# A decoder trunk on one core: output projections that hold the activations and move 512 weight columns, and norms with tokens on partitions

## The chip, the core and the metric

The kernel runs on one core of a Trainium2 chip. The metric is the device time of one execution in microseconds, taken as the median of several runs. The engines are TensorE (PE, with its weight loads as PEld), VectorE (DVE), ScalarE (ACT), GpSimd (POOL), and SyncE (SP), which here only issues DMAs.

## The reference

The input is 256 tokens of 2048 channels in float32. Two post-norm layers follow each other. Each of the four sub-steps has the same frame:

```python
x = layer_norm(alpha * x + mixer(x) @ w_out, g, b)   # alpha = 4 ** 0.25
x = layer_norm(alpha * x + conv_ffn(x), g, b)        # up, causal conv, gate, down
```

The even layer's mixer is a state-space scan beside block-sparse attention; the odd layer's is a three-branch sparse attention beside retention. Both end in a 2048 x 2048 output projection. The feed-forward part is 5632 wide, so its down projection is 5632 x 2048. `layer_norm` takes mean and variance over the 2048 channels of a token, with float32 throughout.

## The kernel before

**Products.** Every float32 operand of a projection is split in a high part and a rest, and three products are summed: high by high, high by rest, rest by high. Activations of a projection lie with channels on partitions, `[128, k, 512]`: 256 tokens of the high part, then 256 of the rest. The weights come from HBM in slabs of up to 128 x 1024 (`prep`); ACT makes the high part (L105, `whi`), DVE the rest (L106, `wlo`). Four buffers each hold the raw slab and the two parts, and slabs are prepared three ahead of their use.

**Forms of a projection.** In form B (`group_b`, L237) the weights stand in TensorE, 128 x 128, and 512 columns of activations move past the high part, 256 past the rest, for two blocks of 128 output channels. In form A (`group_a`, L266 to L268) 128 tokens of activations stand and up to 512 weight columns move, three matmuls for each token half. Form S (`group_one`, L191 to L193) is B for one block of 128 with three moves of 256.

**Output projections and norms.** There are four (`out_proj`): after the even mixer (16 k), the first down projection (44 k), after the odd mixer (16 k), the second down projection (44 k). Each has seven B groups of 256 output channels and two S groups of 128. The residual `r` lies with channels on partitions, so a norm needs sums over partitions: `token_sums` (L345) multiplies by a column of 1/2048, early for the first 15 blocks and once more for the last. `norm` then spreads mean (L359) and inverse deviation (POOL's power, L368, and L359 again) over partitions by transposes, and goes block by block: subtract the mean (L378), scale (L387), high part of `x` on ACT (L401), rest on DVE (L403). The blocks behind the first two are applied inside the next stage's first group (`apply_to`). At norm 3 each block gets its bias on ACT (L396) and is stored (L397), 16 stores of 128 KB.

**Order.** A scheduler orders each engine's instructions from the program order and its own estimates; `Fill` hands small steps to the projections' loops, a few after each k. The DMAs of SP go in one queue in program order. At the start SP issues x in eight pieces between the weight slabs, then the constants (`ident`, `prm`, `tri`, then `oh` at L459 and `mk`), and then more slabs, the sixteenth first; the matmul L463 on `oh` makes the position bias.

## Time and profile before

| | us |
|---|---|
| median of 3 runs | 2350.85 (2349.8 to 2352.26) |
| the profiled execution's span | 2351.1 |
| TensorE busy in it | 2321.1 |
| VectorE busy | 1460.5 |
| ScalarE busy | 1160.9 |
| output projection 0, first matmul to last | 286.59 to 382.89 |
| output projection 1 | 882.67 to 1129.80 |
| output projection 2 | 1490.77 to 1587.22 |
| output projection 3 | 2087.20 to 2334.33 |

The profiled execution lies 0.25 us above the median, so its rows stand for the runs. A row's second number is the length of that row: of one instruction, or of several that follow each other with the same operands, counted by x. Matmuls overlap in the records, so the pace is read from start to start, not from a row's length. An idle time in brackets stands before its row, with what ended it.

### The profile page before, as it was taken

The numbers are of one execution on the slowest core, as the hardware profiler recorded it, in microseconds if no ns is written. First come the engines' busy times: TensorE is split into PE (matmuls) and PEld (weight loads), VectorE is DVE, ScalarE is ACT, GpSimd is POOL, SyncE is SP. The second block draws the span as 40 slices with busy tenths as digits, with TensorE's granted clock in tenths as the row PEclk, the third lists the DMA queues.
The fourth block names the chain that finished last, engine by engine and source line by source line (L and its number), as shares of the span: only waits on it lengthen the run. The fifth ranks groups of instructions, "written<-read, shape, count | busy, mean of one in ns | idle before, by whom it ended". The sixth has DMA issues, their size and how long they took to land.

```text
span 2351.1 us, 34466 instructions
## 1 busy us (share of the span) xinstructions
PE 2321.1 (99%) x13638; PEld 2043.2 (87%) x13638; DVE 1460.5 (62%) x2095; ACT 1160.9 (49%) x1556; POOL 20.8 (1%) x29
## 2 busy tenths in 40 slices
PE   9999999999999999999999999999999999999997
PEld 9888888888888888889789888888888888888887
DVE  5677667766666664555645667768666666655555
ACT  5554544655555554444545553446555555544443
POOL 0001000000000000000000000000000000000000
PEclk9999999999999999999999999999999999999999
DMA  7664554655555555555656634455555555555553
GB/s 239 196 192 148 160 169 145 205 187 188 190 190 185 192 189 191 188 188 178 186 168 223 195 108 153 162 176 168 192 189 189 188 188 188 188 190 190 188 190 112
DMA packets 124674, 426.30 MB, mean 181 GB/s; under 512 B 13872, under 2 KB 18400, under 8 KB 124384
## 3 DMA queue, kind: packets, MB, share of 16 engines
q1 hardware_dynamic: 124512, 424.09, 54.0%
q8 instruction: 107, 1.75, 0.3%
q14 instruction: 55, 0.45, 0.1%
HBM read 421.93 MB, written 2.11 MB: 180 GB/s over the span
## 4 chain that ended last, share of the span: by engine, by line
PE 87%; issue 10%; DVE 1%; DMA 1%; ACT 0%; SPq 0%; POOL 0%; ACTq 0%; POOLq 0%; DVEq 0%
PE acc L237 74%; PE acc L266 2%; PE acc L267 2%; PE acc L268 2%; PE ps L237 1%; PE acc L191 1%; PE acc L192 1%; PE acc L193 1%; PE ps L568 1%; DVE r L387 0%; PE ps L507 0%; DMA wraw<-in_ev_in 0%; PE ps L534 0%; DMA r<-in_x 0%; DMA oh<-in_c_onehot 0%
## 5 line engine op out<-in xcount | busy, mean ns | idle before, releaser
L106 DVE TENSOR_TENSOR wlo<-wraw,whi 128x1024 fp32r<-128x1024 f32 (+4 forms) x818 | 973.2, 1191 | 645.4 <-ACT whi L105 642.7
L105 ACT ACTIVATE whi<-wraw 128x1024 fp32r<-128x1024 f32 (+4 forms) x818 | 843.3, 1032 | 793.0 <-PE acc L237 613.6
L237 PE MATMUL acc<-x,whi 128*128 128x512 f32 x3840 | 1202.6, 399 | 3.4 <-DVE x L403 3.4
L237 PEld LDWEIGHTS acc<-x,wlo 128*128 128x128 f32 x3840 | 707.4, 189 | 158.5 <-issue 0.2
L237 PE MATMUL acc<-x,wlo 128*128 128x256 f32 x3840 | 741.0, 279 | 0.0
L237 PEld LDWEIGHTS acc<-x,whi 128*128 128x128 f32 x3840 | 595.9, 190 | 16.3 <-DVE x L403 3.9
L237 PE MATMUL acc<-g,whi 128*128 128x512 f32 x1232 | 385.3, 396 | 0.0
L237 PEld LDWEIGHTS acc<-g,wlo 128*128 128x128 f32 x1232 | 229.9, 188 | 52.9
L237 PE MATMUL acc<-g,wlo 128*128 128x256 f32 x1232 | 240.4, 278 | 0.0
L237 PEld LDWEIGHTS acc<-g,whi 128*128 128x128 f32 x1232 | 188.8, 189 | 1.2
L280 ACT ACTIVATE tmp<-acc 128x512 f32<-128x512 f32 x120 | 71.6, 596 | 216.2 <-PE acc L237 216.2
L237 PE MATMUL acc<-y,whi 128*128 128x512 f32 x448 | 140.9, 399 | 0.0
L266 PE MATMUL acc<-whi,x 128*128 128x512 f32 (+4 forms) x288 | 101.1, 351 | 1.9 <-ACT x L401 1.1
L267 PE MATMUL acc<-wlo,x 128*128 128x512 f32 (+4 forms) x288 | 100.9, 350 | 0.0
L268 PE MATMUL acc<-whi,x 128*128 128x512 f32 (+4 forms) x288 | 100.3, 349 | 0.0
L237 PEld LDWEIGHTS acc<-y,wlo 128*128 128x128 f32 x448 | 82.0, 188 | 18.0
L237 PE MATMUL acc<-y,wlo 128*128 128x256 f32 x448 | 86.5, 280 | 0.0
L1017 DVE SCALAR_TENSOR_TENSOR c<-fpad,prm,c 128x256 f32<-128x256 f32 x176 | 73.9, 480 | 1.4 <-ACT c L1014 1.3
L237 PEld LDWEIGHTS acc<-y,whi 128*128 128x128 f32 x448 | 69.8, 189 | 1.6 <-DVE y L171 0.2
L283 DVE TENSOR_TENSOR u<-acc,tmp 128x512 f32<-128x512 f32 x44 | 30.5, 693 | 53.7 <-ACT tmp L280 53.7
L266 PEld LDWEIGHTS acc<-whi,x 128*128 128x128 f32 x288 | 55.5, 193 | 7.8 <-ACT x L401 1.5
L283 DVE TENSOR_TENSOR fpad<-acc,tmp 128x512 f32<-128x512 f32 x42 | 29.1, 692 | 51.6 <-ACT tmp L280 51.6
(290 smaller groups left out, 1548.0 us busy)
## 6 DMA issues: line engine op xcount, KB each, us to landing
wraw<-in_up SPq DMA_DIRECT2D x328, 512.0 KB, 3.3
wraw<-in_down SPq DMA_DIRECT2D x174, 512.0 KB, 3.3
wraw<-in_od_in SPq DMA_DIRECT2D x96, 512.0 KB, 3.5
wraw<-in_ev_in SPq DMA_DIRECT2D x72, 512.0 KB, 3.6
wraw<-in_ev_out SPq DMA_DIRECT2D x32, 512.0 KB, 3.5
wraw<-in_od_out SPq DMA_DIRECT2D x32, 512.0 KB, 3.3
wraw<-in_up SPq DMA_DIRECT2D x32, 384.0 KB, 3.0
wraw<-in_ev_in SPq DMA_DIRECT2D x16, 348.0 KB, 4.3
```

Source lines behind the costliest of these rows:

```text
L105: a = nc.scalar.activation(hi[:, :n], raw[:, :n], AF.Copy)
L106: b = nc.vector.tensor_tensor(lo[:, :n], raw[:, :n], hi[:, :n].bitcast(F32), op=OP.subtract)
L191: nc.tensor.matmul(acc, hi[:, kk, :], xh, start=(k == 0), stop=False)
L192: nc.tensor.matmul(acc, hi[:, kk, :], xl, start=False, stop=False)
L193: nc.tensor.matmul(acc, lo[:, kk, :], xh, start=False, stop=(k == nk - 1))
L237: nc.tensor.matmul(acc, wt, mv, start=(k == 0 and i < len(unit)), stop=(k == nk - 1 and i >= len(unit)))
L266: nc.tensor.matmul(o, xh, wh, start=(k == 0), stop=False)
L267: nc.tensor.matmul(o, xh, wl, start=False, stop=False)
L268: nc.tensor.matmul(o, xl, wh, start=False, stop=(k == KT - 1))
L280: nc.scalar.activation(t, a[:, :, 256:], AF.Copy, scale=sign)
L283: nc.vector.tensor_tensor(d, a[:, :, :256], t, op=OP.add)
L1017: nc.vector.scalar_tensor_tensor(c[:, i, :], pad[:, i, t:t + 256], w[:, t:t + 1], c[:, i, :], op0=OP.mult, op1=OP.add)
```

## The change

All four output projections go in four groups of 512 output channels, in form A: the activations of 128 tokens stand, 512 weight columns move, three matmuls for each token half and k. The residual `r` now has tokens on partitions, `[128, 2, 2048]`, and is loaded for that in one DMA of 2 MB, which SP issues behind `tri` and ahead of `oh`, `mk` and the slabs that follow. A group's evacuation is one addition per token half (L485, L487) with a partial statistic (L489, bn_stats), and the norm merges these (L188), makes the inverse deviation (L189 on DVE, L190 on POOL) and centres and scales 512 channels at once (L204).

In a projection's last group the last four slabs (8 k) are first multiplied for token half 0 only. Half 0's norm is issued then, and half 1 of the four slabs follows on TensorE. The normed values are turned to channels on partitions by transposes (`turn`, L238), four of 128 x 128 for each token half and 512 channels, 32 per norm. For the first 512 channels the evacuation is ACT (L247, high part) and DVE (L248 and L249, rest) per 128 channels; for the others ACT writes 4 x 128 (L253) and DVE makes high part and rest of all four at once (L255, L256). A table, `plan`, sets between which matmuls each turn stands: two in the half-1 pass, the others in the next stage's head, its first 8, 4 or 8 slabs, which are multiplied for half 0's tokens, then half 1's, then with the weights' rests (`head_b`). The head's slabs are prepared during the projection's groups, into memory that is free at that time (`home`). For norms 1 to 3 the residual `r` is first given its gain and bias again from rows broadcast to all partitions (8 DMAs per norm, two DVE operations of 128 x 1024 per group, L509 and L510). At norm 3 the blocks go by DVE (L214, L215) or by ACT and POOL (L223 to L225) to eight stores of 256 KB (L207).

```diff
+LEAD = 4
...
 def out_jobs(src, nk):
-    return [(src, "B", cols((256 * i, 256)), nk) for i in range(7)] + [
-        (src, "S", cols((1792 + 128 * i, 128)), nk) for i in range(2)]
+    return [(src, "A", cols((512 * i, 512)), nk) for i in range(4)]
...
+        self.plan = {("t1", LEAD - 2): [(0, 0)], ("t1", LEAD - 1): [(0, 1)]}
+        if idx in (0, 2):
+            self.plan.update({("h0", head - 3): [(1, 0)], ("h0", head - 1): [(1, 1)], ("h1", 1): [(0, 2)],
+                              ("h1", 4): [(0, 3)], ("h1", head - 1): [(1, 2)], ("lo", 3): [(1, 3)]})
...
+    def start(self, t):
+        T, nc = self.k, self.k.nc
+        mv, rs = self.mv[:, t, :], self.rs[:, t, :]
+        nc.vector.bn_aggr(mv, self.stats[:, t, :, :])
+        nc.vector.tensor_scalar(rs[:, 0:1], mv[:, 1:2], EPS, None, op0=OP.add)
+        nc.gpsimd.tensor_tensor(out=rs[:, 1:2], in0=rs[:, 0:1], in1=T.mhalf[:, 0:1], op=OP.pow)
+        if self.idx == 3:
+            nc.vector.tensor_scalar(self.nm[:, t:t + 1], mv[:, 0:1], rs[:, 1:2], -1.0, op0=OP.mult, op1=OP.mult)
+            self.finish_pool(t, 2 + t)
+            if t == 1:
+                self.finish(0, 3)
+            for c in range(2 + t):
+                self.finish(t, c)
+        else:
+            self.centre(t, 0)
+            self.centre(t, 1)
...
+    def turn(self, t, c):
+        T, nc = self.k, self.k.nc
+        if c > 1:
+            self.centre(t, c)
+        ps = T.ps()
+        for i in range(4):
+            nc.tensor.transpose(ps[:, 128 * i:128 * i + 128], T.r[:, t, 512 * c + 128 * i:512 * c + 128 * i + 128], T.ident)
+        g, b = T.lng[:, self.idx, :], T.lnb[:, self.idx, :]
+        x = T.x[:, 4 * c:4 * c + 4, :]
+        hi, lo = (x[:, :, 256 * j + 128 * t:256 * j + 128 * t + 128] for j in range(2))
+        y = T.rp.tile([128, 2, 256], F32, name="tmp", bufs=2).rearrange("p a (b c) -> p (a b) c", b=2)
+        if c == 0:
+            for i in range(4):
+                k = 4 * c + i
+                p = ps[:, 128 * i:128 * i + 128]
+                nc.scalar.activation(hi[:, i, :], p, AF.Identity, scale=g[:, k:k + 1], bias=b[:, k:k + 1])
+                nc.vector.tensor_scalar(y[:, i, :], p, g[:, k:k + 1], b[:, k:k + 1], op0=OP.mult, op1=OP.add)
+                nc.vector.tensor_tensor(lo[:, i, :], y[:, i, :], hi[:, i, :].bitcast(F32), op=OP.subtract)
+            return
+        for i in range(4):
+            k = 4 * c + i
+            nc.scalar.activation(y[:, i, :], ps[:, 128 * i:128 * i + 128], AF.Identity, scale=g[:, k:k + 1],
+                                 bias=b[:, k:k + 1])
+        nc.vector.tensor_copy(hi, y)
+        nc.vector.tensor_tensor(lo, y, hi.bitcast(F32), op=OP.subtract)
...
+        for t in range(2):
+            for k in range(n):
+                for u in order:
+                    for o, acc in enumerate(units[u]):
+                        c = 256 * u + 128 * o
+                        nc.tensor.matmul(half(acc, t), slabs[k][0][:, 0, c:c + 128], half(act[k], t),
+                                         start=(k == 0 and t == 0), stop=False)
+                self.turns.at(f"h{t}", k)
+        for k in range(n):
+            for u in order:
+                for o, acc in enumerate(units[u]):
+                    c = 256 * u + 128 * o
+                    nc.tensor.matmul(acc[:, :256], slabs[k][1][:, 0, c:c + 128], act[k][:, :256], start=False, stop=False)
+            self.turns.at("lo", k)
...
+    def three(self, o, a, t, wh, wl, first, last):
+        nc = self.nc
+        xh, xl = a[:, t * 128:(t + 1) * 128], a[:, 256 + t * 128:256 + (t + 1) * 128]
+        nc.tensor.matmul(o, xh, wh, start=first, stop=False)
+        nc.tensor.matmul(o, xh, wl, start=False, stop=False)
+        nc.tensor.matmul(o, xl, wh, start=False, stop=last)
...
+        for s in range(n):
+            if s == drain:
+                self.fill.flush()
+            if step:
+                step(s)
+            hi, lo = w.get(first + s)
+            for kk in range(2):
+                k = 2 * s + kk
+                for t in range(2 if s < n - lead else 1):
+                    self.three(acc[:, t, :], act[k], t, hi[:, kk], lo[:, kk], k == 0, k == nk - 1)
+                self.fill.pop()
+            if s >= n - lead:
+                held.append((s, hi, lo))
+        if idx:
+            self.fill.flush()
+        if not last:
+            self.add(g, idx, acc, slice(0, 2))
+            return
+        norm = Norm(self, idx, self.stats)
+        self.add(g, idx, acc, slice(0, 1))
+        norm.start(0)
+        for i, (s, hi, lo) in enumerate(held):
+            for kk in range(2):
+                k = 2 * s + kk
+                self.three(acc[:, 1, :], act[k], 1, hi[:, kk], lo[:, kk], False, k == nk - 1)
+            norm.at("t1", i)
+        self.add(g, idx, acc, slice(1, 2))
+        norm.start(1)
+        self.turns = norm
...
+            at = [(1, 3), (1, 5), (1, 7), (2, 1), (2, 3), (2, 5), (2, 7), (3, 1)]
+        else:
+            at = [(3, 9), (3, 11), (3, 13), (3, 15)]
...
+        r = self.r[:, ts, 512 * g:512 * g + 512]
+        if idx:
+            nc.vector.tensor_tensor(r, r, acc[:, ts, :], op=OP.add)
+        else:
+            nc.vector.scalar_tensor_tensor(r, r, ALPHA, acc[:, ts, :], op0=OP.mult, op1=OP.add)
+        for t in range(ts.start, ts.stop):
+            nc.vector.bn_stats(self.stats[:, t, g, :], self.r[:, t, 512 * g:512 * g + 512])
...
+            5, lambda: nc.vector.scalar_tensor_tensor(r, r, ALPHA, ap[0], op0=OP.mult, op1=OP.mult),
+            2, lambda: nc.vector.scalar_tensor_tensor(r, ap[1], ALPHA, r, op0=OP.mult, op1=OP.add))
...
         self.load_consts()
-        for c in range(4):
-            p = self.r[:, 4 * c:4 * c + 4, :]
-            self.fill.add(lambda p=p: nc.vector.tensor_scalar(p, p, ALPHA, None, op0=OP.mult))
+        nc.sync.dma_start(self.r, self.I["tokens"].rearrange("(t p) c -> p t c", t=2))
         self.bias_scratch()
```

TensorE round norm 0, before (`y` are the mixer's outputs, `whi` and `wlo` the weight parts, `tmp` the squares, `lnst` the statistics, `x` the normed activations):

```order
L193 MATMUL acc<-y,wlo 128x256
L345 MATMUL ps<-inv_dm,r 128x1 x2
L345 MATMUL ps<-inv_dm,tmp 128x1 x2
L359 MATMUL ps<-ident,lnst 128x128 x4
L237 MATMUL acc<-x,whi 128x512 x2
L237 MATMUL acc<-x,wlo 128x256 x2
```

The same place after (`A` holds the mixer's outputs, `B` the head's slabs):

```order
L353 MATMUL acc<-whi,A 128x512
L238 MATMUL ps<-ident,r 128x128 x4
L351 MATMUL acc<-whi,A 128x512
L352 MATMUL acc<-wlo,A 128x512
L353 MATMUL acc<-whi,A 128x512
L351 MATMUL acc<-whi,A 128x512
L352 MATMUL acc<-wlo,A 128x512
L353 MATMUL acc<-whi,A 128x512
L238 MATMUL ps<-ident,r 128x128 x4
L337 MATMUL acc<-x,B 128x2x128 x2
L337 MATMUL ps<-x,B 128x2x128 x2
```

The sums and spreads have gone; half 0's first two turns stand in the half-1 pass, one ahead of the last slab and one behind it, and the head follows at once.

VectorE at norm 0, before (from the last S group's evacuation on):

```order
L311 TENSOR_TENSOR r<-acc,r 128x256
L354 TENSOR_TENSOR lnst<-ps,lne 128x4
L365 SCALAR_TENSOR_TENSOR lnst<-lnst 128x1 x2
L378 TENSOR_TENSOR r<-r,ps 128x256
L367 TENSOR_SCALAR lnst<-lnst 128x2
L378 TENSOR_TENSOR r<-r,ps 128x256 x3
L387 SCALAR_TENSOR_TENSOR r<-r,prm,ps 128x256 x2
L378 TENSOR_TENSOR r<-r,ps 128x256
L403 SCALAR_TENSOR_TENSOR x<-r,prm,x 128x256
```

VectorE at norm 0, after (from half 0's addition on; L109 is the weights' rest, L106 of before):

```order
L487 SCALAR_TENSOR_TENSOR r<-r,acc 128x512
L489 BN_STATS st_3049<-r 128x6
L188 BN_AGGR mv<-st_3049 128x2
L189 TENSOR_SCALAR rs<-mv 128x1
L204 TENSOR_SCALAR r<-r,mv,rs 128x512 x4
L109 TENSOR_TENSOR wlo<-wraw,whi 128x768 x3
L248 TENSOR_SCALAR tmp<-ps,prm 128x128
L487 SCALAR_TENSOR_TENSOR r<-r,acc 128x512
L249 TENSOR_TENSOR x<-tmp,x 128x128
L489 BN_STATS st_3049<-r 128x6
L248 TENSOR_SCALAR tmp<-ps,prm 128x128
```

All four blocks of half 0 are centred in a row, and three weight rests and half 1's addition stand ahead of the first 128 channels' rest (L249).

SP at the start, the difference (a minus is before, a plus after; the names are the constants, the tokens and the even in-projection's slabs):

```order
-L419 DMA tri<-in_c_tri 128x128
-L459 DMA oh<-in_c_onehot 32x384
-L461 DMA mk<-in_c_late 8x384
+L518 DMA ident<-in_c_ident 128x128
+L518 DMA prm<-in_params 128x916
+L518 DMA tri<-in_c_tri 128x128
+L1167 DMA r<-in_tokens 128x2x2048
+L554 DMA oh<-in_c_onehot 32x384
+L556 DMA mk<-in_c_late 8x384
 L102 DMA wraw<-in_ev_in 128x696
```

The tokens stand ahead of `oh`, `mk` and every slab from the sixteenth on. On TensorE the matmul on `oh` (L558, before L463) now stands 40 matmuls later than before.

## Rows read from the trace of the kernel before

**Rows 1.** The page, part 1: busy time, share of the span and instructions of each engine.

```profile
PE 2321.1 (99%) x13638; PEld 2043.2 (87%) x13638; DVE 1460.5 (62%) x2095; ACT 1160.9 (49%) x1556; POOL 20.8 (1%) x29
```

**Rows 2.** The page, part 4: the chain that ended last, by engine.

```profile
PE 87%; issue 10%; DVE 1%; DMA 1%; ACT 0%; SPq 0%; POOL 0%; ACTq 0%; POOLq 0%; DVEq 0%
```

**Rows 3.** The timeline of TensorE inside down0, two k of one group of 256 columns: start us, us, engine, line, operation, out<-in, count.

```profile
900.09 0.63 PE L237 MATMUL acc<-g,whi 128*128 128x512 f32 x2
...
900.56 0.39 PE L237 MATMUL acc<-g,wlo 128*128 128x256 f32 x2
...
900.79 0.63 PE L237 MATMUL acc<-g,whi 128*128 128x512 f32 x2
```

**Rows 4.** The timeline of TensorE at the end of down1, the last k's of a group of 128 columns.

```profile
2333.97 0.28 PE L193 MATMUL acc<-g,wlo 128*128 128x256 f32 x1
...
2334.33 0.28 PE L193 MATMUL acc<-g,wlo 128*128 128x256 f32 x1
```

**Rows 5.** The timeline of TensorE in the odd layer's first in-projection (`group_a`: 512 weight columns move), the first and the last of a stretch: 120 matmuls lie from the first row's start to the last row's.

```profile
1145.02 0.39 PE L266 MATMUL acc<-whi,x 128*128 128x512 f32 x1
...
1172.22 0.39 PE L266 MATMUL acc<-whi,x 128*128 128x512 f32 x1
```

**Rows 6.** The timeline round norm 0: the end of the projection, the early sums, the norm's chain and the next stage's first matmul. Brackets give the idle time before a row and what ended it.

```profile
380.69 0.95 PE L345 MATMUL ps<-inv_dm,bc 128*128 128x1 f32 x8
...
381.50 0.36 PE L191 MATMUL acc<-y,whi 128*128 128x256 f32 x1
...
382.89 0.28 PE L193 MATMUL acc<-y,wlo 128*128 128x256 f32 x1
...
385.87 0.16 DVE L367 TENSOR_SCALAR lnst<-lnst 128x2 f32<-128x2 f32 x1
...
386.11 0.69 POOL L368 TENSOR_TENSOR lnst<-lnst,mhalf 128x2 f32<-128x2 f32 x1 [154.09 <-DVE lnst L367]
...
389.02 1.22 PE L237 MATMUL acc<-x,whi 128*128 128x512 f32 x2 [1.69 <-DVE x L403]
```

**Rows 7.** The same two rows at norms 1 and 2: last matmul of the projection, first of the stage behind it.

```profile
1129.80 0.28 PE L193 MATMUL acc<-g,wlo 128*128 128x256 f32 x1
...
1136.40 0.79 PE L266 MATMUL acc<-whi,x 128*128 128x512 f32 x1 [1.11 <-ACT x L401]
...
1587.22 0.28 PE L193 MATMUL acc<-y,wlo 128*128 128x256 f32 x1
...
1593.31 1.22 PE L237 MATMUL acc<-x,whi 128*128 128x512 f32 x2 [1.69 <-DVE x L403]
```

**Rows 8.** Windows behind the norms 0, 1 and 2 and over the end: busy time (and count) of PE, PEld, DVE, ACT, POOL, then granted clock, DMA share, GB/s.

```profile
389.00:393.90 4.90, 4.88 (x15) 4.11 (x16) 3.82 (x11) 2.78 (x6) 0.00 (x0) 0.50 0.25 80
...
1136.40:1141.40 5.00, 5.00 (x12) 3.94 (x13) 4.62 (x11) 2.49 (x5) 0.00 (x0) 0.50 0.92 324
...
1593.30:1598.80 5.50, 5.49 (x17) 4.72 (x18) 4.20 (x12) 3.38 (x8) 0.00 (x0) 0.50 0.23 72
2334.50:2351.00 16.50, 2.03 (x13) 1.35 (x12) 11.20 (x32) 8.17 (x18) 4.12 (x6) 0.65 0.37 128
```

**Rows 9.** Groups of instructions with shapes apart: busy us, mean ns of one | idle before, releaser.

```profile
L106 DVE TENSOR_TENSOR wlo<-wraw,whi 128x1024 fp32r<-128x1024 f32 x742 | 907.5, 1224 | 605.3 <-ACT whi L105 603.0 <-ACT y L170 1.5
L106 DVE TENSOR_TENSOR wlo<-wraw,whi 128x768 fp32r<-128x768 f32 x32 | 30.6, 955 | 2.0 <-ACT whi L105 1.8
L105 ACT ACTIVATE whi<-wraw 128x768 fp32r<-128x768 f32 x32 | 27.1, 846 | 23.6 <-PE ps L237 14.6 <-PE acc L192 5.5 <-issue 3.5
L297 DVE TENSOR_TENSOR r<-acc,r 128x512 f32<-128x512 f32 x28 | 19.4, 692 | 19.6 <-PE acc L237 19.6
L724 DVE TENSOR_SCALAR L<-ps,acum 128x128 f32<-128x128 f32 x16 | 5.5, 343 | 0.0
L973 DVE BATCH_NORM_STATS2 gn<-ps 128x6 f32<-128x128 f32 x16 | 4.1, 289 | 1.6 <-PE ps L968 1.6
L975 DVE BATCH_NORM_AGGREGATE gn<-gn 128x2 f32<-128x6 f32 x16 | 2.5, 172 | 0.0
L376 POOL TENSOR_TENSOR r<-r,tmp 128x256 f32<-128x256 f32 x5 | 3.5, 732 | 0.0
```

**Rows 10.** Transposes of 128x128 f32 on TensorE in the mixers: their group (columns as in rows 9), and a row of the timeline with two.

```profile
L534 PE MATMUL ps<-ident,z 128*128 128x128 f32 x72 | 11.5, 276 | 0.0
...
301.19 0.38 PE L534 MATMUL ps<-ident,z 128*128 128x128 f32 x2
```

**Rows 11.** The timeline of the end: the issues of the 16 output stores, first to last.

```profile
2339.54 9.04 SPq L397 DMA_DIRECT2D out_dram<-r  x16
```

**Rows 12.** The timeline of the start round the bias matmul L463, the first matmul at the wider spacing behind it and the first at the old one again, and one window of the same stretch (columns as in rows 8).

```profile
25.39 0.43 SPq L459 DMA_DIRECT2D oh<-in_c_onehot  x1
...
28.38 0.32 PE L266 MATMUL acc<-whi,x 128*128 128x352 f32 x1
...
30.08 0.80 PE L463 MATMUL ps<-oh,prm 32*8 32x384 f32 x2 [1.38 <-DMA oh<-in_c_onehot]
32.24 0.49 PE L266 MATMUL acc<-whi,x 128*128 128x344 f32 x1
...
35.65 0.32 PE L266 MATMUL acc<-whi,x 128*128 128x344 f32 x1
...
25.00:30.00 5.00, 3.71 (x24) 3.42 (x22) 3.59 (x6) 2.16 (x3) 0.00 (x0) 1.00 0.97 333
```

409 lines of the change are left out of this document (202 added, 207 removed).

## The prediction

> **What bounds the kernel now.** I read the page's first part first: TensorE is busy in 2321.1 of 2351.1 us [rows 1]. The chain that ended last is 87% TensorE, and its 10% "issue" lies between matmuls that follow each other with nothing in between [rows 2]. So three things can move the end: the pace of the matmuls, the places where TensorE stands still or runs at the half clock, and what lies behind the last matmul. VectorE and ScalarE have slack on average, but not at the norms, where TensorE waits for them. I therefore read the timeline for the pace of each form [rows 3 to 5], then the norms [rows 6 to 8], the end [rows 11] and the start [rows 12]. The profiled execution lies 0.25 us above the median of the runs, so what I add to its span I take as added to the median.
>
> **Pace of the projections.** In form B one k of 256 output channels takes 900.79 - 900.09 = 0.70 us (0.698 as a mean over the stage); the two wide matmuls are 0.23 each, the two half ones 0.115 [rows 3]. In form S three matmuls take 2334.33 - 2333.97 = 0.36 us for 128 channels [rows 4]. A k of 2048 channels is thus 7 x 0.698 + 2 x 0.36 = 5.61 us. Form A is in the trace, in another projection: 1172.22 - 1145.02 = 27.2 us for 120 matmuls, 0.2267 each [rows 5]. The new k is 4 groups x 2 halves x 3 = 24 of these, 5.44 us. The gain is 0.165 us per k, and over 16 + 44 + 16 + 44 = 120 k it is **-19.8 us**. Its cover is the supply of weights: a slab of 2 k in form A lasts 12 x 0.2267 = 2.72 us, and its rest takes DVE 1.22 [rows 9], so supply stays ahead. The bounds: if the form ran at 0.233 a matmul, the pace of B's wide ones, a k would cost 5.59 and the gain were 1.9 us; if it runs as in rows 5, 19.8. The nearest row is the one of the same form, so I take 19.8.
>
> The Trainium skill (TensorE: Matmul & The Clock Gate, "Wait — 56ns, not 53.3ns?") gives a matmul of N columns N/2.4 ns and a fixed 2.5 ns, that is 215.7 and 109.2 ns for 512 and 256. By that rule B and S together would be 5.20 us per k, A 5.18, and the change would gain about 3 us in all. The rows disagree: 0.2267 for A's 512 columns, 0.233 for B's, 0.12 for 256.
>
> **The three inner norms, before.** From the projection's last matmul to the next stage's first there are 389.02 - 382.89 - 0.12 = 6.0 us [rows 6], 6.5 and 6.0 [rows 7]. The early sums took 0.8 out of TensorE's row at each [rows 6]. Then the granted clock is 0.50 for 4.9, 5.0 and 5.5 us [rows 8]: at the lower of its two levels (1.2 GHz against 2.4), after TensorE had mostly stood still, and half of each stretch is lost, 2.45, 2.5 and 2.75. The sum is 9.3 + 9.8 + 9.5 = 28.6 us.
>
> **The same norms after**, counted from the end of half 0's pass in the last group. TensorE has 8 k x 3 x 0.2267 = 5.44 us of half 1 and two turns of four transposes at about 0.11 (one takes 0.28 on average, two in a row 0.38 [rows 10]), so it wants the first normed k at 6.3 us. DVE's order decides when it gets it. The addition of 128 x 512 is 0.69 [rows 9]; bn_stats is in the trace only at 128 columns, 0.289, the merge 0.172 [rows 9]. For bn_stats at 512 columns I take the addition's 0.69. With L189 the statistics are done at 2.1. POOL's power is 0.69 and began 0.08 behind its input [rows 6]; with 0.3 for the way it ends at 3.1. Four centres of 128 x 512 (an estimate of 0.48 each, 0.39 back to back, between the 0.343 of L724 at 128 columns from PSUM and the 0.69 of an addition [rows 9]) end at 4.8. Behind them in DVE's row stand three weight rests of 768 columns, 0.87 each back to back [rows 9]: 7.4. Then L248 (0.35), half 1's addition (0.69) and L249 (0.28, as bn_stats at its width): the first k is there at 8.5, and TensorE has stood 2.1 us. The second k needs bn_stats, L248, the merge, another rest and L249: 10.5, where 0.7 us of matmuls of the first k cover less than half; 1.3 more. The third and fourth cost 0.6 together. That is 4.0 us of standing at norms 0 and 2; at norm 1, by the same count, 3.6. To it come 32 transposes x 0.11 = 3.6, and the head's three narrow passes (0.120 per 256 columns as in rows 4, where half of a wide one is 0.116; 144 of them), 0.6 at norms 0 and 2. For the clock I take what a stop of 1.4 us cost at the start: from 32.24 to 35.65 the matmuls ran at twice the spacing, half of it lost, 1.7 [rows 12]. The sum is 10.0 + 8.9 + 10.0 = 28.9 us, so **+0.3** against before. From below: no standing and no half clock, 3 x 3.6 + 1.3 = 12.1, a gain of 16.5. From above: twice the standing (11.7 more) and the 6.8 us at half clock that before has, 3.4 instead of 1.7 (5.1 more), a loss of 17. The estimate lies near the middle and I take it. The residual's two DVE operations per group and its 8 DMAs lie beside the projection's matmuls, where DVE has 2.72 - 1.22 = 1.5 us free per slab; I cost them at nothing. Without that cover a group's two, about 1.3 us each, would be 2.6 us.
>
> **The end.** Before, the last matmul starts at 2334.33 and the span ends at 2351.1, 16.65 us behind its end [rows 4, 11]; the early sums cost 0.8. After: half 0's norm (to 3.1 us) and three of its blocks on DVE (six operations at 0.6 back to back) end at 6.9, where half 1's matmuls have long been done (5.44). Half 1's addition, statistics, power and three blocks on DVE end at about 13.3; the blocks on ACT and POOL (POOL at 0.73 per 256 columns [rows 9], so 2.9 for two operations of 512) end beside that. From the last store's issue, 2348.6, to the span's end were 2.5 us [rows 11]. So 16 us from half 0's end, 10.5 behind the last matmul: -6.1, with the sums **-6.9**. If POOL or the larger store is slower it is -3; if the chain is tighter, -9.
>
> **The start.** 2 MB of tokens now stand in SP's queue ahead of `oh` and the later slabs. The queue moved 333 GB/s with the DMA engines busy to 0.97 at that time [rows 12], so what is behind is late by 6.3 us. `oh` was issued at 25.39 and L463 ran at 30.08 [rows 12]; now it would at about 36.3. TensorE comes there 40 matmuls later than before, at 0.155 each (24 in 3.71 us [rows 12]) and a little more, at about 34.9, and waits 1.4; the sixteenth slab costs another 1.1. Before it waited 1.38 there with 1.7 of half clock behind. With a second stop and its half clock I take **+3**, from 0 (the tokens overlap as well as the slabs do) to 7 (all 6.3 uncovered).
>
> The Trainium skill (DMA: Bandwidth & Descriptors, "Queues, rings and completion order") states that each DMA engine takes the descriptors of a ring in order. By that rule, too, what stands behind the tokens waits for their bytes; the trace before has no load of 2 MB to show it.
>
> **The sum:** -19.8 + 0.3 - 6.9 + 3 = -23.4 us; 2350.85 - 23.4 is about 2327 us.
>
> **The rivals.**
> - *The turns are covered.* The scheduler has put each turn between matmuls, and if DVE gets ahead at the norms, only the transposes and the narrow passes remain: 16.8 us less, 2310. For it: DVE is busy 62% on average [rows 1]. Against: three weight rests stand ahead of L248 in its order, and an engine takes its row in order.
> - *The norms or the start are dearer than counted* by half of their bounds, 8 to 18 us: 2335 to 2345. For it: the half clock of 6.8 us that each norm before had [rows 8], and a turn that comes late stops the turns behind it.
> - *Form A runs no faster here than B.* If its pace is 0.233 as in rows 3, the gain of 19.8 shrinks to 1.9 and the time is 2345. Against: rows 5, where the same form ran beside the same weight loads and splits. The skill's fixed-cost rule above (Trainium skill, TensorE: Matmul & The Clock Gate) would give 2344, almost the same case, and I count it in it.
> - *Slower: DVE's row at the norms.* The weight rests wait for ACT's high parts, these for buffers that the held last four slabs free only as half 1 is multiplied; L248 and L249 stand behind them, and so do the later turns. Each rest then comes with TensorE's own pace, the head starves, and TensorE runs at half clock through the head. The end goes above 2351 if each of the three norms costs 23.4 / 3 = 7.8 us more than counted, that is 17.5 us each. What speaks against: the held slabs are freed 1.36 us apart, ACT takes 0.85 for each [rows 9], and DVE reaches the rests only at 4.8.
> - *The change doesn't take.* The matmul order shows that it does on TensorE; no chance is kept for it.
>
> **How the numbers follow.** The forecast's own range is 2319 to 2335, chance 0.58. The turns covered, 2305 to 2318: 0.20. Dearer norms or start, 2335 to 2345: 0.12. Form A at B's pace: 0.04. Slower by DVE's row: 0.06. A time within 0.2% (4.7 us, about what a measurement of this kernel can tell from no change) of 2350.85 would be 2346.2 to 2355.6; half of the last two cases falls there, 0.05, and 0.05 lies above. Faster holds 0.90. The range of 8 in 10 reaches from 2311 to 2341: it leaves out the lower part of the covered case and the upper part of the dearer ones.
>
> **What would show it right or wrong.** In the profile after: a spacing of 0.227 between the projections' matmuls (0.233 would mean the fourth rival). At norm 0 a stop of about 2 us before the head's first matmul, ended by DVE's L249, smaller stops behind it, and a granted clock of 0.50 for some 3 us (no stop: the turns are covered; more than 17 us lost in all: DVE's row). About 10.5 us from the last matmul to the end. At the start TensorE waits for `oh` at about 35 us. The sum would be wrong if a stage that the change does not touch changes its pace, which no row before can show.

## The result, and the profile after

The changed kernel takes 2325.72 us (median of 4 runs, 2325.32 to 2326.42) against 2351.56 (4 runs) for the kernel before: a ratio of 0.9892, 95% interval 0.9878 to 0.9906. The forecast was 2327 with a range of 2311 to 2341. The sum was met; several of its terms were not.

In the changed kernel a run's time lies about 1.8 us above its span: the runs of 2325.32 and 2326.42 have spans of 2323.5 and 2324.6. In the kernel before it lies 2.0 to 3.8 us above (22 runs beside the experiments, with spans of 2347.8 to 2350.8, median 2349.6). The profiled execution of before, with its span of 2351.1, is thus a run of about 2353 and lies some 2 us above the median that the prediction started from, not 0.25 as it said. Stages are compared below by spans of single executions, so about 1.5 of the 27.6 us between the two spans belong to this execution of before and not to the change.

The page after, parts 1 and 4, against [rows 1, 2]:

```profile
PE 2298.9 (99%) x12550; PEld 1983.5 (85%) x12550; DVE 1441.5 (62%) x1978; ACT 1130.0 (49%) x1503; POOL 28.7 (1%) x36
...
PE 65%; issue 32%; DVE 1%; DMA 1%; POOL 0%; ACT 0%; DVEq 0%; POOLq 0%; SPq 0%
```

TensorE is still busy in 99% of the span; it is the span that has become shorter. What it lost is matmul time: 22.2 of the 27.6 us. The chain's share of "issue", time in which the engine waited for nothing that the profile shows, has grown from 10 to 32%; nothing below rests on it. The next table cuts the span at first matmuls of the stages, as the timeline gives them. "Again" is a second profiled execution of the same changed kernel (span 2325.9), taken among the experiments.

| stage | before | after | again |
|---|---|---|---|
| start, up to the first form-B matmul | 57.98 | 55.68 | 58.89 |
| output projection 0, norm 0, up projection 0 | 596.08 | 593.59 | 592.85 |
| output projection 1, norm 1, form-A part of the odd in-projection | 367.19 | 357.30 | 357.23 |
| output projection 2, norm 2, up projection 1 | 596.43 | 592.98 | 592.92 |
| output projection 3 and the end | 263.9 | 254.8 | 254.8 |
| the two parts that the change leaves alone | 469.52 | 469.15 | 469.15 |

The pace first. These are the first matmuls of groups 0 and 1 of down0, in the timeline of TensorE (answers to [rows 3, 4]):

```profile
877.92 0.39 PE L351 MATMUL acc<-whi,A 128*128 128x512 f32 x1
...
937.78 0.39 PE L351 MATMUL acc<-whi,A 128*128 128x512 f32 x1
```

44 k of 512 channels take 59.86 us, 1.360 per k, and four groups 5.44: the predicted value to the last digit. So the pace gives 0.165 us x 16 = 2.64 us in the small projections and 7.26 in the large ones, 19.8 in all. Taking that out of the table leaves for the norms 0, 1 and 2, with all else in their stages: +0.15, -2.63 and -0.81 us (again: -0.59, -2.70, -0.87), for the end -1.8 (-1.8), for the start -2.30 (+0.91).

Norm 0 in the timeline (answers to [rows 6]; PE L353 and L351 are the projection, L238 the turn, L337 the head):

```profile
371.42 0.39 PE L353 MATMUL acc<-whi,A 128*128 128x512 f32 x1
371.85 0.69 DVE L487 SCALAR_TENSOR_TENSOR r<-r,acc 128x512 f32<-128x512 f32 x1 [3.12 <-PE acc L353]
...
372.59 0.50 PE L351 MATMUL acc<-whi,A 128*128 128x512 f32 x1 [0.78 <-DVE r L487]
...
376.25 2.69 DVE L109 TENSOR_TENSOR wlo<-wraw,whi 128x768 fp32r<-128x768 f32 x3
...
378.86 0.41 DVE L248 TENSOR_SCALAR tmp<-ps,prm 128x128 f32<-128x128 f32 x1
379.18 0.68 DVE L487 SCALAR_TENSOR_TENSOR r<-r,acc 128x512 f32<-128x512 f32 x1
...
379.77 0.29 DVE L249 TENSOR_TENSOR x<-tmp,x 128x128 fp32r<-128x128 f32 x1
...
380.16 0.47 PE L337 MATMUL acc<-x,B 128*128 128x256 f32 x2 [0.94 <-ACT x L247]
...
382.30 0.77 PE L337 MATMUL acc<-x,B 128*128 128x256 f32 x2 [1.18 <-DVE x L249]
```

DVE's row runs as foreseen: addition, statistics, centres, three rests up to 378.9, L248, half 1's addition, L249, and TensorE's head behind it (its bracket names ACT's L247; L249 ends at 380.06, 0.10 ahead of the head). TensorE stands three times: 0.94 us right behind half 0's pass (from 371.65, where the matmul of 371.42 is done at its spacing, to 372.59; the first matmul of half 1 waits for L487), 0.94 ahead of the head, and 1.18 ahead of the second k. The first was not foreseen. In the second execution these stops last 0.94, 0.92 and 1.19, and a fourth of 0.30 follows; norm 2 is alike, and norm 1 has 0.94, 0.98 and 0.25.

The granted clock in windows at the norms 0, 1 and 2, first in the first profile, then in the second (columns as in rows 8, which they answer):

```profile
382.00:386.00 4.00, 3.70 (x19) 3.73 (x20) 3.55 (x11) 0.46 (x1) 0.60 (x1) 0.57 0.39 121
1120.00:1124.00 4.00, 3.10 (x13) 2.58 (x14) 4.00 (x13) 2.77 (x8) 0.00 (x0) 1.00 0.85 302
1572.00:1576.00 4.00, 2.61 (x19) 2.17 (x19) 3.77 (x12) 1.74 (x5) 0.42 (x1) 1.00 0.69 230
```

```profile
384.00:388.00 4.00, 2.51 (x18) 2.08 (x17) 3.56 (x12) 1.45 (x4) 0.60 (x1) 1.00 0.60 210
...
1122.00:1126.00 4.00, 3.02 (x13) 2.21 (x12) 4.00 (x12) 3.22 (x8) 0.00 (x0) 1.00 0.88 321
1574.00:1578.00 4.00, 2.75 (x18) 2.31 (x18) 4.00 (x12) 2.10 (x6) 0.06 (x1) 1.00 0.74 249
```

The half clock of 5 us or more that followed each norm before is gone, except for 3.4 us at norm 0 in the first profile (a mean of 0.57 over the 4 us of its window). At norms 1 and 2, and at all three in the second execution, the clock stays at 1.00, though at norm 2, and at norm 0 of the second execution, TensorE stands for as long.

The end (answers to [rows 11]; L214 and L215 are DVE's two operations per output block, L224 and L225 GpSimd's):

```profile
2306.62 2.44 DVE L214 SCALAR_TENSOR_TENSOR r<-r,mv,x 128x512 f32<-128x512 f32 x2
2306.73 13.46 SPq L207 DMA_DIRECT2D out_dram<-r  x8
2306.97 1.54 POOL L224 TENSOR_TENSOR r<-r,x 128x512 f32<-128x512 f32 x1 [1.18 <-ACT r L223]
...
2308.59 1.59 POOL L225 TENSOR_TENSOR r<-r,x 128x512 f32<-128x512 f32 x1
...
2308.98 2.41 DVE L215 SCALAR_TENSOR_TENSOR r<-r,rs,x 128x512 f32<-128x512 f32 x2
2311.32 0.68 DVE L485 TENSOR_TENSOR r<-r,acc 128x512 f32<-128x512 f32 x1
...
2317.43 2.41 DVE L215 SCALAR_TENSOR_TENSOR r<-r,rs,x 128x512 f32<-128x512 f32 x2
```

DVE's operations come in pairs of 2.4 us while GpSimd is at work, a mean of 1.2 each, not the 0.6 that the prediction took. The mean hides two lengths. Taken one by one in the trace, one operation of each pair lasts 0.74 us and the other 1.75; the long one starts while a GpSimd product runs and ends 0.54 to 0.56 us behind the product's end. Of the twelve operations four are long. The last matmul started at 2308.92 and the span ends at 2323.5: 14.4 us behind that matmul's end, where 10.5 were predicted and 16.65 were spent before.

### The profile page after: what moved, and what is told of

Read it like the earlier page. It is cut to its first block, busy times and chain, and to the rows that moved or that the text cites. A ratio compares the mean times of both kernels' runs of the same rounds, so it can differ in the third digit from the quotient of the medians.

```text
span 2323.5 us, 32157 instructions
## 1 busy us (share of the span) xinstructions
PE 2298.9 (99%) x12550; PEld 1983.5 (85%) x12550; DVE 1441.5 (62%) x1978; ACT 1130.0 (49%) x1503; POOL 28.7 (1%) x36
## 4 chain that ended last, share of the span: by engine, by line
PE 65%; issue 32%; DVE 1%; DMA 1%; POOL 0%; ACT 0%; DVEq 0%; POOLq 0%; SPq 0%
PE acc L312 37%; PE acc L353 8%; PE acc L351 8%; PE acc L352 8%; PE ps L663 1%; DMA wraw<-in_ev_in 1%; DVE wlo L109 0%; PE ps L602 0%; PE acc L337 0%; PE ps L629 0%; PE ps L1150 0%; PE ps L601 0%; POOL rs L190 0%; PE ps L312 0%; PE ps L238 0%
## 5 line engine op out<-in xcount | busy, mean ns | idle before, releaser
L109 DVE TENSOR_TENSOR wlo<-wraw,whi 128x1024 fp32r<-128x1024 f32 (+4 forms) x796 | 950.6, 1198 | 617.6 <-ACT whi L108 616.4
L312 PE MATMUL acc<-x,whi 128*128 128x512 f32 x3776 | 1178.4, 397 | 0.0
L351 PE MATMUL acc<-whi,A 128*128 128x512 f32 x512 | 201.3, 393 | 1.6 <-DVE r L487 0.8
L353 PE MATMUL acc<-whi,A 128*128 128x512 f32 x512 | 199.4, 390 | 0.0
L352 PE MATMUL acc<-wlo,A 128*128 128x512 f32 x512 | 199.4, 390 | 0.0
L351 PE MATMUL acc<-whi,B 128*128 128x512 f32 x448 | 174.6, 390 | 1.6 <-DVE r L485 1.6
L353 PE MATMUL acc<-whi,B 128*128 128x512 f32 x448 | 174.3, 389 | 0.0
L352 PE MATMUL acc<-wlo,B 128*128 128x512 f32 x448 | 174.3, 389 | 0.0
L351 PEld LDWEIGHTS acc<-whi,A 128*128 128x128 f32 x512 | 96.2, 188 | 21.9 <-DVE r L487 1.2
L353 PEld LDWEIGHTS acc<-whi,A 128*128 128x128 f32 x512 | 96.2, 188 | 20.2 <-DVE A L272 0.3
L352 PEld LDWEIGHTS acc<-wlo,A 128*128 128x128 f32 x512 | 96.3, 188 | 19.5
L351 PEld LDWEIGHTS acc<-whi,B 128*128 128x128 f32 x448 | 84.1, 188 | 19.7 <-DVE r L485 2.4
L352 PEld LDWEIGHTS acc<-wlo,B 128*128 128x128 f32 x448 | 84.1, 188 | 17.5
L353 PEld LDWEIGHTS acc<-whi,B 128*128 128x128 f32 x448 | 84.1, 188 | 17.4
L351 PE MATMUL acc<-whi,x 128*128 128x512 f32 (+4 forms) x272 | 93.0, 343 | 0.3 <-ACT V L685 0.3
L353 PE MATMUL acc<-whi,x 128*128 128x512 f32 (+4 forms) x272 | 92.8, 341 | 0.0
```

The costliest lines, as they stand in the source:

```text
L109: nc.vector.tensor_tensor(lo[:, :n], raw[:, :n], hi[:, :n].bitcast(F32), op=OP.subtract)
L312: nc.tensor.matmul(acc, wt, mv, start=(k == 0 and i < len(unit)), stop=(k == nk - 1 and i >= len(unit)))
L351: nc.tensor.matmul(o, xh, wh, start=first, stop=False)
L352: nc.tensor.matmul(o, xh, wl, start=False, stop=False)
L353: nc.tensor.matmul(o, xl, wh, start=False, stop=last)
```

## The experiments

Every variant computes the whole reference, from the changed kernel with one edit (two with several). Times are medians of 4 or 5 runs; the kernel before had medians of 2351.7 to 2351.9 beside them. They were taken in three series, and differences from `r_after` are in part across series.

**The changed kernel again, and the tokens' place.** `r_after` is the changed kernel without an edit. `e4_tokens_late` moves one DMA:

```diff
         self.load_consts()
-        nc.sync.dma_start(self.r, self.I["tokens"].rearrange("(t p) c -> p t c", t=2))
...
             self.group_a(self.xk, ev_v(680))
+            tok = nc.sync.dma_start(self.r, self.I["tokens"].rearrange("(t p) c -> p t c", t=2))
+            self.tc.keep_in_program_order(tok)
```

> The changed kernel as it is, once more, beside the others of this group. It says how far its stages differ from one profiled execution to the next: the first projection lasted 47.3 us in its first profile and 47.3 to 51.0 in four variants that leave it alone, the third output projection 94.2 and 94.2 to 96.0. Theory: these differences belong to the execution (where TensorE's clock falls or a load lands late), not to the variants; then this profile shows other values than the first one in one or both stages, and its median lies within 1 us of 2325.7. Rival: they belong to the variants' orders; then its stages are as in its first profile, within 0.2 us.

> The 2 MB of tokens are loaded behind the first two groups of the even in-projection instead of ahead of the one-hot constant, the late mask and the slabs behind them. The order of SP and the place of the bias matmul are then those of the kernel before (40 matmuls earlier on TensorE). Theory: the start gained because the tokens' place moved the bias matmul back in TensorE's order, to where its constant has landed; with the tokens away the matmul is early again, TensorE stands for about 1.4 us there, the half clock follows, and the first projection lasts 50.5 us again, 3 us more than in the changed kernel: about 2328 to 2329. Rival: the start gained by VectorE's four rescalings of the residual that are gone, and the tokens cost time in the queue; then this is the same or 1 to 2 us faster, 2324 to 2326.

Measured: 2326.24 and 2325.71 us. The bias matmul in the first profile of the changed kernel, in the second with a window of the clock behind it, and with the tokens late:

```profile
35.98 0.80 PE L558 MATMUL ps<-oh,prm 32*8 32x384 f32 x2
```

```profile
37.83 0.80 PE L558 MATMUL ps<-oh,prm 32*8 32x384 f32 x2 [2.73 <-DMA wraw<-in_ev_in]
...
39.00:42.00 3.00, 3.00 (x12) 3.00 (x12) 1.94 (x3) 1.71 (x3) 0.00 (x0) 0.50 0.35 97
```

```profile
29.94 0.80 PE L558 MATMUL ps<-oh,prm 32*8 32x384 f32 x2 [0.49 <-DMA tri<-in_c_tri]
```

One and the same kernel stood 0.2 us at this matmul in one execution (by the spacing of its neighbours; the profile gives no bracket) and 2.73 in the next, with 3.4 us at the clock's half level behind it, 3.00 of them in the window: the constant landed 9.6 us after its issue in the first, 10.6 in the second (4.6 before). The eleven profiled executions with the tokens ahead in the queue (these two and nine variants) stood there for 0.2 to 2.7 us, so this stage says nothing on the variants. With the tokens late there was 0.49, and the start ended at 56.30, in the midst of 55.6 to 58.9. My theory of `e4` (3 us more) has fallen: the matmul's old place costs no more than its new one, and the tokens' place is worth nothing that these runs tell. The third projection of `r_after` was as in its first profile; the 1.4 to 1.8 us more that three variants had there (`e1`, `e3` and `e5`; `e8` later 0.4) did not come back, and I leave them open.

**The end on VectorE alone.**

```diff
-            nc.vector.tensor_scalar(self.nm[:, t:t + 1], mv[:, 0:1], rs[:, 1:2], -1.0, op0=OP.mult, op1=OP.mult)
-            self.finish_pool(t, 2 + t)
-            if t == 1:
-                self.finish(0, 3)
-            for c in range(2 + t):
+            for c in range(4):
                 self.finish(t, c)
```

> At norm 3 all eight blocks of the output go by VectorE (L214, L215); the two that went by ScalarE and GpSimd (L223 to L225) no longer do. In the changed kernel VectorE's two-input operations of 128x512 took 0.74 us when alone and 1.2 us each (2.44 for two) while GpSimd ran its products. Theory: the two engines hold each other up where both read SBUF, so VectorE loses more than GpSimd takes off it. Then 16 operations go at 0.6 to 0.7 us each instead of 12 in 12.7 us, and the end comes 2 to 3 us earlier: 14.6 us behind the last matmul become about 12, the whole about 2323. Rival: these operations take 1.2 us for their operands' sake, whatever GpSimd does; then four more of them make the end 4 to 5 us later, about 2330.

Measured: 2324.12 us, 2.1 below `r_after`, with no run in common (2322.88 to 2324.83 against 2325.68 to 2327.66; the kernel before had 2351.90 and 2351.91 beside them). DVE's rows at the end of this variant (L210 and L211 are L214 and L215):

```profile
2306.59 1.40 DVE L210 SCALAR_TENSOR_TENSOR r<-r,mv,x 128x512 f32<-128x512 f32 x2
...
2307.91 1.41 DVE L211 SCALAR_TENSOR_TENSOR r<-r,rs,x 128x512 f32<-128x512 f32 x2
...
2317.66 1.41 DVE L211 SCALAR_TENSOR_TENSOR r<-r,rs,x 128x512 f32<-128x512 f32 x2
```

Each lasts 0.74 or 0.75 us, 0.66 from start to start. The eight operations of a token half span 5.4 us, where six spanned 6.7, and from the last matmul's start to the span's end 12.2 us instead of 14.6. The variant without a lead (below) has the same operation once alone and once beside GpSimd:

```profile
2326.85 0.75 DVE L214 SCALAR_TENSOR_TENSOR r<-r,mv,x 128x512 f32<-128x512 f32 x1
...
2327.20 1.52 POOL L224 TENSOR_TENSOR r<-r,x 128x512 f32<-128x512 f32 x1 [1.17 <-ACT r L223]
...
2327.57 1.69 DVE L214 SCALAR_TENSOR_TENSOR r<-r,mv,x 128x512 f32<-128x512 f32 x1
```

0.75 and 1.69 us for the same 128x512. The Trainium skill (SBUF — State Buffer, "SBUF: two separate sides") says that VectorE operations with two SBUF inputs and GpSimd operations that read SBUF lock a shared pair of ports against each other, and that the loser waits for the whole instruction. The rows agree in kind: the long operation ends at 2329.26, 0.54 us behind the end of the product that ran when it started, and lasts 0.94 longer than alone. The variant with half the lead (below) shows beside one product an addition with an input in PSUM (`acc`) and, behind it, an operation with both inputs in SBUF:

```profile
2312.34 1.52 POOL L224 TENSOR_TENSOR r<-r,x 128x512 f32<-128x512 f32 x1 [1.17 <-ACT r L223]
2312.66 0.68 DVE L485 TENSOR_TENSOR r<-r,acc 128x512 f32<-128x512 f32 x1
2313.26 1.16 DVE L215 SCALAR_TENSOR_TENSOR r<-r,rs,x 128x512 f32<-128x512 f32 x1
```

The addition took the 0.68 us that it also takes with GpSimd idle; the other one was held until 0.56 us behind the product's end. In the trace of before GpSimd's block of products at the end lay beside DVE operations with one input in PSUM, which kept their length too (0.42 us for 128x256).

**Half 1 in an accumulator of its own.**

```diff
         acc = self.acc_pool.tile([128, 2, 512], F32, name="acc")
+        other = self.ps() if g == 3 else acc[:, 1, :]
...
-                    self.three(acc[:, t, :], act[k], t, hi[:, kk], lo[:, kk], k == 0, k == nk - 1)
+                    self.three((acc[:, 0, :], other)[t], act[k], t, hi[:, kk], lo[:, kk], k == 0, k == nk - 1)
...
-                self.three(acc[:, 1, :], act[k], 1, hi[:, kk], lo[:, kk], False, k == nk - 1)
+                self.three(other, act[k], 1, hi[:, kk], lo[:, kk], False, k == nk - 1)
...
```

> In the last group of each projection half 1 gets an accumulator tile of its own. In the changed kernel TensorE stands for 0.94 us behind half 0's pass until VectorE has read half 0's sums, though half 1's matmuls write another bank. Theory: the stop comes of both halves being parts of one tile; with two tiles it is gone at all four places. But the first normed k is made by VectorE's chain, which starts at half 0's end as before, so the stop ahead of the head grows by about as much, and the end (VectorE's chain too) does not move: 0 to 1.5 us less in all. Rival: the stops cost what they last, 4 x 0.94, and the time falls by 3 to 4 us, to about 2322.

Measured: 2325.29 us. Norm 0, where half 0's pass ends and where the head begins:

```profile
374.04 0.39 PE L353 MATMUL acc<-whi,A 128*128 128x512 f32 x1
374.27 0.39 PE L351 MATMUL ps<-whi,A 128*128 128x512 f32 x1
...
382.17 0.47 PE L337 MATMUL acc<-x,B 128*128 128x256 f32 x2 [1.41 <-ACT x L247]
```

The stop is gone (0.23 us from one matmul to the next), so it came of the shared tile, and the stop ahead of the head has grown from 0.94 to 1.41; the two behind it are 0.81 and 1.16. Against `r_after` the table's three norm stages differ by -0.1, 0.0 and 0.0 us, and the end by 0.0. The rival (3 to 4 us) has fallen: a stop ahead of a chain that runs on another engine was free, at the norms and at the end.

**The weight rests held back.** The three slabs behind the head are prepared at the head's second k, their DVE instruction pinned behind what stands ahead in the program:

```diff
...
                 self.turns.at(f"h{t}", k)
+                if (t, k) == (0, 1):
+                    w.pump(first + n + 3, pin=True)
...
```

> The weight rests (L109) of the three slabs behind the head are held back on VectorE until the head's second k, so that they no longer stand ahead of L248 and L249 of the first turn. Nothing else is changed. Theory (of the prediction): these rests set when TensorE gets its first normed k. Then the head's first matmul follows the turn at once at norms 0 and 2 (0.9 to 1.0 us of standing gone), the stop ahead of the second k shrinks from 1.2 to about 0.8, and the half clock at norm 0 (3 us, 1.5 lost) may go too: 4 to 6 us less in all, 2320 to 2322. Rival 1: ScalarE's high part and half 1's addition set it, and the rests only fill the gap: under 1 us. Rival 2: the held rests come too late for the body behind the head, and TensorE stops there: slower.

Measured: 2325.00 us. Norm 0 (L339 is the head, L240 a turn, L206 a centre, L249 ScalarE's high part):

```profile
379.17 0.47 PE L339 MATMUL acc<-x,B 128*128 128x256 f32 x2
...
380.93 0.48 PE L339 MATMUL acc<-x,B 128*128 128x256 f32 x2 [0.71 <-DVE x L251]
...
382.93 0.63 PE L240 MATMUL ps<-ident,r 128*128 128x128 f32 x4 [0.34 <-DVE r L206]
...
384.05 0.47 PE L339 MATMUL acc<-x,B 128*128 128x256 f32 x2 [0.49 <-ACT x L249]
...
384.28 2.69 DVE L109 TENSOR_TENSOR wlo<-wraw,whi 128x768 fp32r<-128x768 f32 x3
```

The head follows at once and the second stop is 0.71, as expected; but a turn of half 1 now waits 0.34 for its centre and the next matmul 0.49 for the turn. From the projection's first matmul to the last of the head there are 118.0 us at norm 0, against 118.2 in `r_after` (both without half clock). Rival 1 holds in its number, though not in its reason: what DVE did not do ahead of the head it did in it, and TensorE waited there. I had named the rests as what sets the stop; they only had their turn in a row that is full: in the changed kernel DVE is busy for 9.78 of the 9.80 us from 374.4 to 384.2 at norm 0, and for 4.00 of 4.00 in the windows at norm 1 above.

**Less work for VectorE in the turns, and all three edits together.**

```diff
-        if c == 0:
-            for i in range(4):
...
-            return
         for i in range(4):
             k = 4 * c + i
             nc.scalar.activation(y[:, i, :], ps[:, 128 * i:128 * i + 128], AF.Identity, scale=g[:, k:k + 1],
```

> The first 512 channels of each half are evacuated like the others: ScalarE writes 4 x 128 and VectorE makes high part and rest of all four at once (about 1.1 us) instead of eight operations of 128 columns (about 2.7 us). Holding the weight rests back moved the stops of TensorE without making the norms shorter, so: Theory: VectorE's whole work between half 0's end and the last turn sets the sum of the stops (it is busy at 1.00 from 375 to 384 in the changed kernel at norm 0). With 1.6 us less of it per turn the norms get 1 to 1.6 us shorter each, though the first normed k comes about 1 us later (all four come at once): 3 to 5 us less in all, about 2321. Rival: the first k's latency sets it; then the norms get up to 1 us longer each, 2326 to 2329.

> Three variants together: the output's blocks all on VectorE, the three weight rests held back behind the head's second k, and the first 512 channels evacuated like the others. Theory (VectorE's work sets the norms, the two engines' contention the end): the end gains 2.3 us as when changed alone, the norms 3 to 5 as from the fewer operations, the held rests nothing: 2318 to 2321. Rival (latency): the end's 2 us alone, and the norms lose up to 3: 2324 to 2327.

Measured: 2325.29 and 2324.59 us. In `e6` the stages from projection 0 to the last matmul of its head take 117.46 us (118.17 in `r_after`), those of norm 2 117.63 (118.25), those of norm 1 357.75 (357.11): -0.7, -0.6 and +0.6. Neither side had it: with fewer operations norms 0 and 2 gain about half of what I expected (the four k come together, and TensorE stands 1.94 us once ahead of the head instead of 0.92 and 1.19), and at norm 1 there is a loss. By their times `e6` and `r_after` cannot be told apart (2323.55 to 2326.49 against 2325.68 to 2327.66). `e7` came out in its rival's range (2324 to 2327): the end is as in `e1`, norm 1 loses 0.95, and at norm 0 the clock fell behind a stop of 1.92 us, as it did not in `e6` behind 1.94.

**The lead: halved, and taken away.** `e5` has `LEAD = 2`. `e9`:

```diff
-        lead = LEAD if last else 0
+        lead = 0
...
-        for i, (s, hi, lo) in enumerate(held):
-            for kk in range(2):
-                k = 2 * s + kk
-                self.three(acc[:, 1, :], act[k], 1, hi[:, kk], lo[:, kk], False, k == nk - 1)
+        for i in range(LEAD):
             norm.at("t1", i)
```

> LEAD is 2 instead of 4: the last two slabs (4 k, 2.72 us) instead of four are kept for half 1, so half 0 leads by 2.72 us less. Theory: with four held slabs the lead is spent on VectorE, where three rests stand in the way; with two, buffers come free earlier, two of the rests are made ahead of the norm, and the norms cost about the same (within 1.5 us each). The end is VectorE's chain from half 0's end on, which comes 2.72 us nearer to the end: 2.7 us more. In all 2 to 5 us more, 2328 to 2331. Rival: the cover of 8 k is what hides the norm, and each of the three inner norms gets 2.7 us longer as well: 10 to 11 us more, about 2336, with half clock 2340.

> No half leads: both token halves of the last four slabs are multiplied slab by slab as in the rest of the projection, and half 0's norm is issued when half 1 is done too; the turns stand in the same order, the first two right behind the projection. Theory: VectorE's chain from a half's last matmul to the first turn takes about 5 us (addition 0.7, statistics 0.7, merge, power 1.0, centre 0.5) and as much again to the first normed k; with nothing beside it TensorE stands 6 to 8 us at each inner norm instead of 2 to 3, and the half clock follows the longer stop at each (1.5 to 3.4 us lost): 6 to 8 us more per norm. The end starts 6.4 us nearer to the last matmul: 5 us more. In all 20 to 28 us more, 2346 to 2354, so that nearly the whole gain of the change is gone. Rival: as with two held slabs instead of four, the norms cost the same within 1 us, since the weight rests are then made ahead: only the end's 3 to 5 us more, about 2330.

Measured: 2329.57 and 2343.09 us, 3.3 and 16.9 above `r_after`. With half the lead the stages of the three norms are 1.0, 0.6 and 1.8 us longer (the last with the irregular third projection in it), the end 1.1. The total is in the expected range (2 to 5), its make-up is not: 2.7 us were expected at the end alone. There DVE now takes half 1's addition between half 0's blocks (2312.66 in the rows shown with `e1`), and from half 0's end to the span's end there are 19.3 us instead of 20.9. Without a lead they are 4.9, 4.9 and 3.9 us longer and the end 4.3. TensorE at norm 0 without a lead, and the clock there:

```profile
377.88 0.39 PE L353 MATMUL acc<-whi,A 128*128 128x512 f32 x1
...
383.08 1.97 PE L238 MATMUL ps<-ident,r 128*128 128x128 f32 x8 [4.82 <-DVE r L204]
...
385.93 0.77 PE L337 MATMUL acc<-x,B 128*128 128x256 f32 x2 [0.88 <-ACT x L247]
...
382.00:391.00 9.00, 7.04 (x32) 6.67 (x33) 7.95 (x23) 3.94 (x11) 1.07 (x2) 0.50 0.14 44
```

TensorE stands 4.82 us ahead of the first turn and 0.88 behind it, and the granted clock is 0.50, the lower of its two levels, over all 9 us of the window. At norms 1 and 2 it stands 5.07 and 4.82 us, and half clock follows there too (6.8 us each). The mechanism is the theory's; its price, 20 to 28 us, was put too high. So of the change's 25.7 us about 17 hang on the lead, though the pace alone gives 19.8: without a lead the new norms cost more than the old ones. The first 4 k of the lead bring four times what the last 4 do.

**The width of a matmul.** Each matmul of the output projections in two:

```diff
                 for t in range(2 if s < n - lead else 1):
-                    self.three(acc[:, t, :], act[k], t, hi[:, kk], lo[:, kk], k == 0, k == nk - 1)
+                    for c in range(0, 512, 256):
+                        self.three(acc[:, t, c:c + 256], act[k], t, hi[:, kk, c:c + 256], lo[:, kk, c:c + 256], k == 0 and c == 0, k == nk - 1 and c == 256)
...
```

> In the output projections each matmul of 512 weight columns is made as two of 256 behind the same standing activations; nothing else is changed. Theory (the pace term of the prediction): a matmul costs more than its columns, 0.120 us for 256 where 512 take 0.2267; 48 x 0.120 = 5.76 us per k instead of 5.44, and over 120 k 38 us more, about 2364: slower than the kernel before, whose B form moves 512 columns for half of its matmuls. Rival: the columns alone set the pace, and the form's gain comes from elsewhere (the weights' supply, the evacuations): the same as the changed kernel, 2326. The Trainium skill's fixed cost (TensorE: Matmul & The Clock Gate, Wait — 56ns, not 53.3ns?) of 2.5 ns per matmul would give 24 x 120 x 2.5 ns = 7 us more, 2333.

Measured: 2362.76 us, 36.5 above `r_after` (38 expected), a ratio to before of 1.0049 (1.0032 to 1.0066). In down0 of this variant:

```profile
899.81 0.28 PE L353 MATMUL acc<-whi,A 128*128 128x256 f32 x1
...
900.89 0.28 PE L353 MATMUL acc<-whi,A 128*128 128x256 f32 x1
```

Nine matmuls in 1.08 us, 0.120 each, where 512 columns take 0.2267: two of them 13.3 ns longer than one of 512. The pace term is shown from both sides: the columns alone do not set it, and the form with 256 columns is slower than the kernel before. Each added matmul brings its weight load with it (15430 loads against 12550), so the price is that of a matmul with its load; which of the two it comes from stays open. The Trainium skill (TensorE: Matmul & The Clock Gate, "Wait — 56ns, not 53.3ns?") has a fixed cost of 2.5 ns per matmul, from which an estimate of 7 us followed; these matmuls do not bear it out.

**A version that beats both.** The output's blocks on DVE alone, and the first 512 channels evacuated like the others at norms 0 and 2 only (`if c == 0 and self.idx == 1:`).

> The output's blocks all on VectorE, and the first 512 channels evacuated like the others at norms 0 and 2 alone (at norm 1, where the head multiplies in form A, this cost 0.6 us). From the stages of the variants that had one of these: the end 2.3 us less, norms 0 and 2 some 0.6 us less each: 3.5 us below the changed kernel, about 2322.5 beside its 2326.2. Rival: the start and the clock at a norm differ by up to 4 us between executions, and no difference beyond that can be told: 2324 to 2326.

Measured: 2322.92 us (2321.13 to 2323.53), ratio to before 0.9876 (0.9861 to 0.9891). Its runs all lie below those of the changed kernel in both series (lowest 2325.32). They overlap with those of `e1`, so that the second edit adds anything is shown by stages alone: in the profiled execution norm 0 and the end are 0.7 and 2.4 us shorter than in `r_after`, and at norm 2 there are 3.4 us of half clock, which `r_after` does not have.

## Why the prediction was right, and where it was not

- **Pace (-19.8).** Right: 5.44 us per k in the trace, 36.5 us back when the width is halved. The rival of form A at B's pace has fallen. So has the estimate of 2344 us from the fixed 2.5 ns of the Trainium skill (TensorE: Matmul & The Clock Gate, "Wait — 56ns, not 53.3ns?").
- **Inner norms (+0.3).** Measured -3.3 and -4.2. The chain on DVE was right to some tenths (L249 ends 8.4 us after half 0's end, 8.5 predicted). The failed step is the half clock: "1.7" at each, from one stop at the start, where six norms in two executions had it once. The stops were counted at 4.0, 3.6 and 4.0 us and are 3.4, 2.2 and 3.4 in the second execution, 0.94 of it at each (the shared tile) that was not foreseen and cost nothing by `e2`; against that, at norms 0 and 2 some 1.4 us of wider spacing between the matmuls were not counted. That the rests are what TensorE waits for was wrong by `e3`: without them the stops move on. The rival "the turns are covered" did not come about: the stops are there.
- **The end (-6.9).** Measured -1.8. The failed step is "0.6 back to back" for DVE's operations, taken from rows without GpSimd beside them. Alone they follow at 0.66 (`e1`), but four of the twelve were held to 1.75 by GpSimd's products, about 4 us in all; `e1`, with four operations more and no product, gives 2.4 us of the 5.1 back. The last store's issue ends at 2320.19 and the span 3.3 us later, where 2.5 were taken. The unforeseen stop of 0.94 has no share: without it (`e2`) the end lasts the same.
- **The start (+3).** Measured -2.3 and +0.9. The delay was right (from issue to landing the constant took 5.1 and 6.0 us more, 6.3 predicted), and TensorE stood 0.2 and 2.7 us for it (1.4 predicted). The failed step is the second stop, "another 1.1" for the sixteenth slab, with a half clock on top of the one that the kernel before has there too: in none of the eleven executions with the tokens ahead does TensorE stand for more than 0.3 us behind the bias matmul. The kernel before stood 1.38 and 0.74 us in its start and lost 1.7 to the half clock; the first execution of the changed kernel lost almost none of this.
- **The sum** of -23.4 was met at -25.8 by medians since the end (5.1 too much gain) offset the norms (about 4 too little) and the start (2 to 5 too little). That it came so near is luck in these three terms. The pace term, three quarters of the whole, carries it. Of the rivals, the slower one (DVE's row) is told apart by the norms: 17.5 us each would have been needed, and they cost less than before.

## What to carry to other kernels

Where a matmul costs more than its columns, count matmuls, each with its weight load, as well as columns: both kernels move 12288 columns per k of an output projection, the one in 34 matmuls, the other in 24. One profiled stage of the same form gives the price. A norm that follows a long sum can be hidden by letting one part of the tokens finish early; the first few microseconds of lead bring most of it, and past that the engine that makes the norm is full, so that moving its work about only moves the stops. Before work is put on GpSimd beside VectorE, look whether both read SBUF: taking it away may be faster.

## What was not expected of the hardware

- The same DVE operation on 128x512 took 0.75 us alone and 1.15 to 1.77 when it started while a GpSimd product ran; it then ended 0.54 to 0.56 us behind the product. An addition with one input in PSUM kept its 0.68 us beside such a product.
- TensorE's clock did not fall at norms 1 and 2 where the engine stood 1.0 us at a time (1.00 in the windows above), and fell at norm 0 in one of two executions of the same program with the same stops. In `e1`, whose inner norms are those of the changed kernel, it fell at norm 2 (3.4 us), and in `e4` at none. Nothing here tells which stop of this length it follows.
- The start of one program ended at 55.68 us in one execution and at 58.89 in another; its constant landed at 35.67 us and at 37.51 behind a load of 2 MB, and only the later landing was followed by half clock.
